# Stores of the experts' results issued from GpSimd instead of ScalarE, in a two-layer mixer with a mixture of experts

## The chip, the cores and the metric

The kernel runs on one core of one Trainium2 chip. The metric is the device time of one execution in microseconds (us); of several executions the median is taken.

## What is computed

The reference is a two-layer network over 256 latent and 256 context tokens of width 1024. Each layer has a mixer (convolution, chunked recurrence, linear recurrence) and then a mixture of 16 experts; the change concerns the mixture alone. Each token has two experts, chosen inside one of four groups:

```python
expert_id = g_sel[:, None] * EXPERTS_PER_GROUP + top_i          # 2 of 16 for each token
combine = jnp.sum(jax.nn.one_hot(expert_id, N_EXPERTS) * top_w[..., None], axis=1)
for e in range(N_EXPERTS):
    ye = (jax.nn.silu(hf @ w_gate[e]) * (hf @ w_up[e])) @ w_down[e]
    y = y + combine[:, e:e + 1] * ye
```

All is float32. One expert has three weight matrices of 2 MB each. Layer 0 sends 512 tokens through the mixture (64 an expert on average), layer 1 only the 256 latent ones (32 an expert).

## The kernel before

**Work of one expert.** `moe(l, hs, fill)` (line 1086) sorts the tokens and then runs a loop over 16 experts (line 1584) in a fixed order. For an expert the kernel multiplies the gathered tokens with the gate and up matrices (`gu`, matmul at line 1356), copies the PSUM result to `gs` (`evac`, line 1373 on ScalarE), transposes and activates it (`act`, lines 1379, 1382, 1391), and multiplies with the down matrix (`down`, line 1404). Each expert has room for 128 tokens in two halves: half 0 holds tokens 0 to 63, half 1 tokens 64 to 127, and work that no token needs is skipped on TensorE by a branch.

**Stores.** For 15 of the 16 experts `store(x, b, ps, n_s)` (line 1466) follows each half of `down`: ScalarE (half 0) or VectorE (half 1) copies PSUM into a tile `Y` (line 1468; three buffers in all), and one or two DMAs write `Y` to the tensor `Yd` in memory (line 1472). That makes three DMAs an expert and 90 over both layers. The first of an expert is always done; the other two carry the condition that the expert has more than `s0` tokens. The number `n_s` is loaded into a register of the issuing engine (line 1597). The DMAs are issued by ScalarE, in its instruction order. The sixteenth expert is kept out of `Yd`.

**Loads.** SyncE (SP) issues all weight loads, in a fixed order (`ahead`, `ewt`, lines 1114 to 1140: a tile of 1 MB at line 1128, two of 512 KB at line 1122), up to 12 tiles ahead in layer 0 and 15 in layer 1. A load waits until TensorE has finished with the tile whose place it takes. It neither reads nor writes `Y` or `Yd`.

**Fetch.** In the last expert's turn `fetch` (line 1543) lets GpSimd issue indirect DMAs that read each token's two rows back from `Yd` (8 in layer 0, 4 in layer 1, line 1554). They need all stores of the layer landed. `take` (line 1566) then weighs and adds the rows (ScalarE line 1570, VectorE lines 1573 and 1575, GpSimd line 1576); `spread_y` (line 1448) and a matmul (lines 1462, 1709) add the sixteenth expert. In layer 1 GpSimd also loads `fin` (line 1589).

**Order.** TensorE's order is the program's own. The order on the other engines is set by a scheduler in the framework, which also places all semaphore waits and hands each DMA the semaphore that tells of its landing.

Of the kernel before, what the change touches and what calls it, by code (L numbers as in the profile page):

```python
# [39 lines left out]
def hybrid_kernel(ctx, tc, x, c, cx, c_ctx, w_mod, b_mod, norm1_g, norm2_g, w_in, conv_w, conv_b, conv_ln_g,  # L40
# [3 lines left out]
    nc = tc.nc  # L44
# [11 lines left out]
    Yd = dram.tile([NE - NPE, P, D], F32, name="Yd", tag="Yd")  # L56
    cnt = [0]

    def bank(shape=(P, 512)):
        cnt[0] += 1  # L60
        return box["ps"].tile(list(shape), F32, tag="ps", name=f"ps{cnt[0]}", bufs=box["nps"])
# [141 lines left out]
    def wsplit(w, a):  # L203
        r = wpair(w, a)
        for hf in range(2):
            whalf(*r, hf)
        return r[1:]
# [878 lines left out]
    def moe(l, hs, fill):  # L1086
# [4 lines left out]
        with tc.tile_pool(name=f"mo{l}", bufs=1, reuse_waits="tile") as mo, \  # L1091
# [7 lines left out]
            def mt(name, shape, dt=F32, tag=None, bufs=1):  # L1099
                return mo.tile(list(shape), dt, name=f"{name}{l}", tag=tag or name, bufs=bufs)  # L1100
# [121 lines left out]
            def onehot(pr):  # L1222
                P2 = tmp.tile([P, NT, 256], F32R, "t4" if last else "q4", f"P2_{l}_{pr}")
                for j in range(2):
                    e = ORDER[2 * pr + j]
                    for i in range(NT):
                        V.tensor_scalar(P2[:, i, j * P:j * P + P], iota1, pm1[:, i, e:e + 1], None, op0=OP.is_equal)
                if last or pr % 2 == 0:
                    XT = tmp.tile([P, KC, 256], F32, "t8", f"XT{l}_{pr}")
                else:  # L1230
                    XT = kt([P, KC, 256], name=f"XT{l}_{pr}", tag="B")
                st[pr] = XT, P2
# [57 lines left out]
            cnti = mt("cnti", [P, NE + 1], I32)  # L1290
# [52 lines left out]
            def load_w(x):  # L1343
                g0, u0, g1, u1, d0, d1 = wt[6 * x:6 * x + 6]
                return [g0, g1, u0, u1, d0, d1]


            def gu(x, b, ps, ws, c=0):
                XT = st[x // 2][0]
                w, q = (64, 512) if b is None else (32, 256)  # L1350
                c0 = (x % 2) * P + (c if b is None else 32 * b)
                o0 = 256 * ((b or 0) % 2)
                for k in range(KC):
                    for t in range(P // w):
                        g, f0 = (t, 0) if b is None else (t // 2, 256 * (t % 2))
                        T.matmul(ps[w * t:w * t + w, o0:o0 + q], XT[:, k, c0:c0 + w],  # L1356
                                 ws[2 * g + k // 4][k % 4][:, f0:f0 + q], start=(k == 0), stop=(k == KC - 1))


            def by32(x, b):  # L1360
                return last and b == 0 if last or x in pec else b == 1

            def evac(x, b, ps):

                gs = tmp.tile([P, 512], F32, "t2", f"gs{l}_{x}_{b}")
                o, src = gs.rearrange("t (h k p) -> t h k p", h=2, k=2), ps.rearrange("t (h p k) -> t h k p", h=2, k=2)
                if x in pec and not by32(x, b):
                    V.tensor_scalar(o, src, Wc[:, x, 2 * b:2 * b + 1], None, op0=OP.mult)  # L1368
                elif x in pec:
                    V.tensor_tensor(o, src, Wc[:, x, 2 * b:2 * b + 2].unsqueeze(2).unsqueeze(3)  # L1370
                                    .to_broadcast([P, 2, 2, P]), op=OP.mult)
                else:
                    S.copy(o, src)  # L1373
                return gs
# [91 lines left out]
            def store(x, b, ps, n_s):  # L1466
                Y = tmp.tile([P, 512], F32, "Y", f"Y{l}_{x}_{b}")
                (V.tensor_copy if b else S.copy)(Y, ps)  # L1468
                w, q = (32, 256) if by32(x, b) else (64, 512)
                for c in range(64 // w):  # L1470
                    s0 = 64 * b + w * c
                    nc.scalar.dma_start(Yd[x, s0:s0 + w, :].rearrange("s (h f) -> h s f", f=q), Y[:, q * c:q * c + q],
                                        **({"cond": n_s > s0} if s0 else {}))

            def overflow():
# [67 lines left out]
            def fetch():  # L1543

                Yf = Yd.rearrange("e s d -> (e s) d")
                for i in range(NT):
                    if last:
                        yas.append(mt(f"ya{i}", [P, 2, D], tag=("vh", "vl")[i]))
                    else:
                        if i % 2 == 0:  # L1550
                            ya = mt(f"ya{i}", [P, 2, 2, D], tag=("vh", "vl")[i // 2])
                        yas.append(ya[:, i % 2])
                    for cc in range(2):
                        G.indirect_dma_start(out=yas[i][:, cc, :], out_offset=None, in_=Yf,  # L1554
                                             in_offset=bass.IndirectOffsetOnAxis(ap=rowi[:, cc, i:i + 1], axis=0),
                                             bounds_check=(NE - NPE) * P - 1, oob_is_err=False)
# [27 lines left out]
            for x in range(NE):  # L1584
                e = ORDER[x]
                ws = load_w(x)
                if last and x == NE - 2:
                    fin = tmp.tile([P, 2, D], F32, "t8", "fin")
                    nc.gpsimd.dma_start(fin[:, 0], final_g.partition_broadcast(P))  # L1589
                pr = x // 2 + 1  # L1590
                more = pr < NE // 2
                if more and x % 2 == 0:
                    onehot(pr)
                n_e = n_next
                wide = x in pec
                if not wide:
                    n_s = nc.values_load(cnti[0:1, e:e + 1], engines=(mybir.EngineType.Activation,), min_val=0,
                                         max_val=NTOK)
                else:
                    fetch()  # L1600
                    if not last:
                        box["w0"] = [wsplit(w_in[1], a) for a in (0, 256)]
                        Z[1:] = [bank()]
                        V.memset(Z[1], 0.0)
                pa = X1 or bank()

                if last:
                    gu(x, 0, pa, ws)
                    if wide:
                        prep(x)  # L1610
                    with tc.If(n_e > 32):  # L1611
                        gu(x, 1, pa, ws)
                else:
                    gu(x, None, pa, ws)
                    if wide:
                        prep(x)
                    else:
                        with tc.If(n_e > 64):
                            gu(x, 2, X2, ws)
                ga = evac(x, 0, pa)  # L1620
                if more:
                    gather(pr, 2 * (x % 2))
                if last or wide:
                    with tc.If(n_e > 64):
                        gu(x, None, X2, ws, 64)
                else:
                    with tc.If(n_e > 96):
                        gu(x, 3, X2, ws)
                gb = evac(x, 1, X2)
                hA = act(x, 0, ga)  # L1630
                hB = act(x, 1, gb)
                if yas:
                    take(*gate((0, 1)))
                if more:
                    gather(pr, 2 * (x % 2) + 1)
                if x + 1 < NE:
                    n_next = count(x + 1)
                if wide:
                    down_w(0, hA, ws)
                    with tc.If(n_e > 64):  # L1640
                        down_w(1, hB, ws)
                elif last:
                    down(0, hA, Y1, ws)
                    with tc.If(n_e > 32):
                        down(1, hA, Y1, ws)
                    store(x, 0, Y1, n_s)
                    with tc.If(n_e > 64):
                        down(None, hB, Y2, ws)
                    store(x, 1, Y2, n_s)
                else:  # L1650
                    py = bank()
                    down(None, hA, py, ws)
                    store(x, 0, py, n_s)
                    with tc.If(n_e > 64):
                        down(0, hB, Y2, ws)
                        with tc.If(n_e > 96):
                            down(1, hB, Y2, ws)
                    store(x, 1, Y2, n_s)
                ahead(x + 1)
                if x == OVER:  # L1660
                    gr = gate_rows(l, 5, mo, "gr", range(NT // 2), NT // 2)
                    overflow()
# [127 lines left out]
```

## Time and profile before

| | |
|---|---|
| median of 3 runs | 1248.26 us (1246.55 to 1252.63) |
| profiled execution | 1250.44 us |
| its span in the trace | 1248.7 us |
| TensorE busy | 1068.6 us, 86% of the span |
| VectorE, ScalarE, GpSimd busy | 541.1, 362.9, 192.9 us |
| expert loop of layer 0, some | 340 to 690 us |
| expert loop of layer 1, some | 957 to 1210 us |

The span is the time from the first to the last instruction of the profiled execution; its own time has 1.7 us more around it. PE is TensorE's matmul, PEld its weight load, DVE is VectorE, ACT ScalarE, POOL GpSimd, SP SyncE; a q behind the name means the engine's sequencer, which issues DMAs and waits without counting as busy. L1472 is line 1472. A tile's buffer number is left out: `w` stands for every weight tile.

### The profile page before, as it was taken

What the parts mean: (1) busy time and instruction counts of PE and PEld (TensorE: products, weight loads), DVE (VectorE), ACT (ScalarE), POOL (GpSimd) and SP (SyncE); (2) the same over time, 40 slices, a digit from 0 to 9 for tenths busy, and PEclk for the clock granted to TensorE, in tenths of its full rate; (3) what the DMA queues carried; (4) which work ended last, traced back from release to release, by engine and by line L of the source; (5) the groups of instructions that cost most, each with busy time, mean ns of one, the idle gap of its engine ahead of it and who ended that gap; (6) DMA issues with size and microseconds to landing.
All of it is one profiled execution on the core that took longest, in us unless ns stands there. A gap on an engine that the chain in (4) does not pass through costs nothing. (4 is left out here: it accounts for less than half of the span.)

```text
span 1248.7 us, 21479 instructions
## 1 busy us (share of the span) xinstructions
PE 1068.6 (86%) x8655; PEld 726.6 (58%) x8655; DVE 541.1 (43%) x1239; ACT 362.9 (29%) x713; POOL 192.9 (15%) x151
## 2 busy tenths in 40 slices
PE   6899798999899899999897498989888968868676
PEld 4577697899654454555343167788776644434332
DVE  3779958832811111111012999937844110111005
ACT  3554255442321111111010354545433221111102
POOL 3411214332000000000002541113420000000012
PEclk9999999999999899999999698989999989988868
DMA  9636642675978787866886452346697989878981
GB/s 317 199 102 201 229 135 69 197 264 194 361 280 318 283 308 281 336 253 251 335 321 244 162 154 68 119 152 210 230 371 279 389 328 400 345 279 333 360 300 72
DMA packets 137304, 313.08 MB, mean 251 GB/s; under 512 B 15700, under 2 KB 101504, under 8 KB 117328
## 3 DMA queue, kind: packets, MB, share of 16 engines
q1 hardware_dynamic: 128896, 295.74, 64.2%
q10 hardware_dynamic: 6048, 8.43, 1.8%
q0 software_dynamic: 2224, 6.95, 1.5%
q8 instruction: 102, 1.67, 0.5%
q14 instruction: 34, 0.28, 0.1%
HBM read 298.25 MB, written 20.71 MB: 255 GB/s over the span
## 5 line engine op out<-in xcount | busy, mean ns | idle before, releaser
L1356 PE MATMUL X<-w,XT 128*32 128x256 f32 (+1 forms) x2016 | 158.1, 432 | 47.4 <-DMA w<-in_w_up_dram 29.0
L1391 DVE TENSOR_TENSOR hT<-sg,ps 128x256 f32<-128x256 f32 x63 | 24.7, 421 | 342.5 <-ACT sg L1382 342.2
L1356 PEld LDWEIGHTS X<-w,XT 128*32 128x32 f32 (+1 forms) x2016 | 78.4, 120 | 124.3 <-issue 45.3
L1356 PE MATMUL ps<-w,XT 128*64 128x512 f32 x512 | 122.7, 619 | 16.4 <-PEq L1478 5.2
L1356 PEld LDWEIGHTS ps<-w,XT 128*64 128x64 f32 x512 | 44.0, 142 | 91.1 <-issue 63.7
L1242 PE MATMUL ps<-P,vh 128*128 128x256 f32 x336 | 88.8, 300 | 4.8 <-PEq L1611 3.5
L1242 PE MATMUL ps<-P,vl 128*128 128x256 f32 x336 | 83.7, 285 | 0.0
L1373 ACT COPY gs<-X 128x512 f32<-128x512 f32 x45 | 26.0, 587 | 192.7 <-PE X L1356 75.8
L756 DVE SCALAR_TENSOR_TENSOR acc<-cb,cwh,acc 128x512 f32<-128x512 f32 (+1 forms) x120 | 81.3, 715 | 1.0
L1242 PEld LDWEIGHTS ps<-P,vh 128*128 128x128 f32 x336 | 65.2, 194 | 21.0 <-issue 10.9
L1468 DVE COPY Y<-Y 128x512 f32<-128x512 f32 x30 | 20.7, 692 | 129.2 <-DMA Yd<-Y 47.5
L1554 POOL DMA_INDIRECT ya<-Yd,rowi x12 | 12.6, 1049 | 388.5 <-issue 357.5
L1242 PEld LDWEIGHTS ps<-P,vl 128*128 128x128 f32 x336 | 65.2, 194 | 0.0
L1404 PE MATMUL Y<-w,hT 128*32 128x256 f32 (+1 forms) x912 | 58.5, 392 | 2.6 <-DMA w<-in_w_down_dram 1.3
L225 PE MATMUL ps<-w,cS 128*32 128x256 f32 x768 | 49.5, 397 | 9.8 <-DMA w<-in_w_mod_dram 9.5
L1404 PE MATMUL ps<-w,hT 128*64 128x512 f32 x240 | 54.8, 598 | 0.4 <-DVE hT L1391 0.3
L1379 PE MATMUL ps<-blob,gs 128*128 128x128 f32 x256 | 41.7, 292 | 12.7 <-ACT gs L1373 7.7
L1373 ACT COPY gs<-ps 128x512 f32<-128x512 f32 x15 | 8.8, 587 | 143.4 <-PE ps L1356 106.8
L1404 PEld LDWEIGHTS Y<-w,hT 128*32 128x32 f32 (+1 forms) x912 | 29.7, 112 | 28.7 <-issue 8.7
L1379 PEld LDWEIGHTS ps<-blob,gs 128*128 128x128 f32 x256 | 28.1, 145 | 28.3 <-ACT gs L1373 17.3
L225 PEld LDWEIGHTS ps<-w,cS 128*32 128x32 f32 x768 | 22.8, 113 | 30.5 <-DMA w<-in_w_mod_dram 10.2
L1589 POOL DMA_DIRECT2D fin<-in_final_g_dram x1 | 0.6, 647 | 250.6 <-ACT gs L1373 250.6
(892 smaller groups left out, 2095.9 us busy)
## 6 DMA issues: line engine op xcount, KB each, us to landing
w<-in_w_down_dram SPq DMA_DIRECT2D x58, 1024.0 KB
w<-in_w_gate_dram SPq DMA_DIRECT2D x49, 1024.0 KB
w<-in_w_mod_dram SPq DMA_DIRECT2D x48, 1024.0 KB
w<-in_w_up_dram SPq DMA_DIRECT2D x48, 1024.0 KB
w<-in_w_in_dram SPq DMA_DIRECT2D x23, 1024.0 KB
w<-in_w_up_dram SPq DMA_DIRECT2D x32, 512.0 KB
w<-in_w_gate_dram SPq DMA_DIRECT2D x30, 512.0 KB
w<-in_w_out_dram SPq DMA_DIRECT2D x8, 1024.0 KB
```

What stands on the lines that cost most here:

```text
L225: T.matmul(ps[32 * j:32 * j + 32, hf * 256:hf * 256 + 256], cS[:, k, :], w[:, k, :], start=(k < 4), stop=(k >= 4))
L756: V.scalar_tensor_tensor(acc[:, ch], src, wcol, acc[:, ch], op0=OP.mult, op1=OP.add)
L1242: T.matmul(ps[:, cc, :], v[:, i, k * P:k * P + P], P2[:, i, :], start=(n == 0), stop=(n == 2 * NT - 1))
L1356: T.matmul(ps[w * t:w * t + w, o0:o0 + q], XT[:, k, c0:c0 + w], ws[2 * g + k // 4][k % 4][:, f0:f0 + q], start=(k == 0), stop=(k == KC - 1))
L1373: S.copy(o, src)
L1379: T.transpose(pt[:, f, :], gs[:, f * P:f * P + P], ident)
L1391: V.tensor_tensor(hT, sg, pt[:, :, 64:128], op=OP.mult)
L1404: T.matmul(ps[w * t:w * t + w, o0:o0 + q], hk, ws[4 + k // 2][k % 2][:, q * t:q * t + q], start=(k == 0), stop=(k == 3))
L1468: (V.tensor_copy if b else S.copy)(Y, ps)
L1554: G.indirect_dma_start(out=yas[i][:, cc, :], out_offset=None, in_=Yf, in_offset=bass.IndirectOffsetOnAxis(ap=rowi[:, cc, i:i + 1], axis=0) ...
L1589: nc.gpsimd.dma_start(fin[:, 0], final_g.partition_broadcast(P))
```

## The change

The 90 stores are issued by GpSimd, and the register with the token count is loaded on GpSimd. Copies, conditions, sizes and addresses stay.

```diff
@@ -1469,7 +1469,7 @@
                 for c in range(64 // w):
                     s0 = 64 * b + w * c
-                    nc.scalar.dma_start(Yd[x, s0:s0 + w, :].rearrange("s (h f) -> h s f", f=q), Y[:, q * c:q * c + q],
+                    nc.gpsimd.dma_start(Yd[x, s0:s0 + w, :].rearrange("s (h f) -> h s f", f=q), Y[:, q * c:q * c + q],
                                         **({"cond": n_s > s0} if s0 else {}))
@@ -1594,7 +1594,7 @@
                 if not wide:
-                    n_s = nc.values_load(cnti[0:1, e:e + 1], engines=(mybir.EngineType.Activation,), min_val=0,
+                    n_s = nc.values_load(cnti[0:1, e:e + 1], engines=(mybir.EngineType.Pool,), min_val=0,
                                          max_val=NTOK)
```

## Rows read from the trace of the kernel before

**Rows 1.** Busy time by stage: start:end, length, busy time (x instructions), granted clock, DMA share, GB/s.
```profile
340.00:690.00 350.00, 318.36 (x2230) 164.95 (x2228) 53.61 (x138) 52.47 (x102) 10.70 (x10) 0.97 0.75 294
...
957.00:1210.00 253.00, 194.30 (x2264) 113.92 (x2264) 34.34 (x76) 41.70 (x86) 1.78 (x3) 0.89 0.86 338
```
**Rows 2.** Waits of PE, 957 to 1210: total us, times, longest us.
```profile
PE X L1356 <- DMA w<-in_w_up_dram: 29.0, 15, 3.6
...
PE ps L1379 <- ACT gs L1373: 4.7, 3, 3.4
...
PE Y L1404 <- DMA w<-in_w_down_dram: 1.3, 1, 1.3
```
**Rows 3.** Waits of PE, 340 to 690.
```profile
PE ps L1356 <- DMA w<-in_w_up_dram: 3.8, 3, 2.1
...
PE ps L1379 <- ACT gs L1373: 2.1, 1, 2.1
...
PE ps L1356 <- DMA w<-in_w_down_dram: 0.3, 1, 0.3
```
**Rows 4.** Waits of SP's queue, 957 to 1210.
```profile
SPq L1128 <- DMA Yd<-Y: 68.8, 7, 13.4
SPq L1122 <- DMA Yd<-Y: 66.1, 7, 16.4
...
SPq L1128 <- DMA w<-in_w_gate_dram: 24.7, 10, 9.2
...
SPq L1122 <- DMA w<-in_w_up_dram: 6.6, 4, 2.3
```
**Rows 5.** Waits of SP's queue, 340 to 690.
```profile
SPq L1128 <- DMA Yd<-Y: 79.9, 5, 17.8
SPq L1122 <- DMA Yd<-Y: 61.6, 5, 18.1
SPq L187 <- DMA Yd<-Y: 21.1, 1, 21.1
```
**Rows 6.** Timeline of SP near the end of layer 1: start, length, instruction.
```profile
1179.39 0.33 SPq L1128 DMA_DIRECT2D w<-in_w_gate_dram  x1
1194.97 1.14 SPq L1122 DMA_DIRECT2D w<-in_w_up_dram  x2
```
**Rows 7.** DMA in 957 to 1210: rate in 40 equal slices; ScalarE's queue.
```profile
GB/s 339 246 420 421 260 424 378 131 311 410 417 420 417 417 402 350 417 400 141 415 421 156 201 318 233 427 417 416 239 394 248 296 424 330 316 395 424 236 286 196
...
q10 hardware_dynamic: 2770, 2.88, 3.3%
```
**Rows 8.** The stores' line: duration ns min/median/max on the issuing queue.
```profile
L1472 ACTq DMA_DIRECT2D Yd<-Y x90: 138/181/6956, 360.3 to 1197.7; - x90
```
**Rows 9.** Timeline of ACT at the end of layer 0's experts.
```profile
653.90 0.59 ACT L1468 COPY Y<-ps 128x512 f32<-128x512 f32 x1 [3.56 <-PE ps L1404]
666.09 4.14 ACTq L1472 DMA_DIRECT2D Yd<-Y  x3
...
682.91 1.15 ACT L1570 ACTIVATE ya<-ya,ws 128x1024 f32<-128x1024 f32 x1 [7.80 <-DMA ya<-Yd,rowi]
```
**Rows 10.** Timeline of POOL, 600 to 700, first and last fetch of layer 0.
```profile
677.14 1.16 POOL L1554 DMA_INDIRECT ya<-Yd,rowi  x1 [354.45 <-issue]
...
686.80 0.99 POOL L1554 DMA_INDIRECT ya<-Yd,rowi  x1 [0.30 <-issue]
```
**Rows 11.** Timeline of PE behind the last expert of layer 0.
```profile
696.95 5.21 PE L1462 MATMUL ps<-yt,PT 128*128 128x512 f32 x8 [14.80 <-DVE yt L1448]
```
**Rows 12.** The fetch's line: duration ns, and time from issue to landing.
```profile
L1554 POOL DMA_INDIRECT ya<-Yd,rowi x12: 987/993/1376, 677.1 to 1212.5; - x12
...
DMA to landing us min/median/max: 5.5/8.8/9.7
```
**Rows 13.** Timeline of POOL in layer 1: a direct DMA issued there.
```profile
1176.89 0.65 POOL L1589 DMA_DIRECT2D fin<-in_final_g_dram  x1 [250.64 <-ACT gs L1373]
```
**Rows 14.** Timeline of ACT at the end of layer 1's experts.
```profile
1226.21 2.19 ACT L1570 ACTIVATE ya<-ya,ws 128x1024 f32<-128x1024 f32 x2
```

## The prediction

> **What bounds the kernel now.** I read the busy time by stage first. In layer 0's expert loop TensorE is busy for 318 of 350 us at a granted clock of 0.97; in layer 1's for only 194 of 253 us at 0.89 [rows 1]. So layer 0 is held by TensorE, and layer 1 by something else. The waits of TensorE name it: in layer 1 three rows of weight loads, 29.0 the largest and 1.3 the smallest, make 38.6 us together, and the copy `gs` on ScalarE 4.7 us [rows 2]. In layer 0 the three load rows make only 6.0 us and `gs` 2.1 [rows 3].
>
> Is the memory path full, then? Its rate in layer 1 is 338 GB/s on average [rows 1], but slice by slice it jumps between some 420 and 131 [rows 7]. A full path would be flat, so the loads are begun too late. The waits of SP's queue tell why. In layer 1, 134.9 us of SP's time end with the landing of a store, `DMA Yd<-Y` (68.8 and 66.1), and six rows that end with an earlier load, 24.7 the first and 6.6 the last, make 72.4 [rows 4]. In layer 0, 162.6 us end with a store [rows 5]. A load touches neither `Y` nor `Yd`. The one tie I see is the framework's landing semaphores: loads of SP and stores of ScalarE seem to get theirs from one set, in turn, and who reuses one waits for its last DMA. One place shows the price: SP issues a load at 1179.39 and the next only at 1194.97 [rows 6].
>
> ScalarE pays too. The last store of layer 0 has its copy done at 654.5 and is issued at 666.09 [rows 9]. The fetch, which needs it landed, starts at 677.14 [rows 10], `take` waits 7.8 us for it [rows 9], and TensorE stands idle for 14.8 us behind the last expert [rows 11].
>
> **The change, part by part.**
>
> 1. *ScalarE loses 90 issues.* The median is 0.18 us, the longest 6.96 [rows 8]. All the path sees of this is `gs` late for TensorE: 4.7 us in layer 1, 2.1 in layer 0 [rows 2, 3]. I take **-6** of 6.8. The cover of the rest is ScalarE's idle time (41.7 us busy of 253 [rows 1]).
>
> 2. *GpSimd gains 90 issues and 30 register loads.* The trace has no store and no conditional DMA there. From below, ScalarE's 0.18 us an issue [rows 8]; from above, 0.65 for a direct load [rows 13] or 1.0 for an indirect one [rows 12]. I take 0.65, the nearest in kind: 2 us an expert, against intervals of some 17 us (253 us for about 15). GpSimd is idle for 354 us before layer 0's fetch [rows 10] and works 1.8 of 253 us in layer 1 [rows 1], so this costs nothing. Without that cover it would be 90 x 0.65 = 58 us. Queued behind a store that waits for its copy are only the next store, `fin` and the fetch; `fin` is not needed before the end.
>
> 3. *SP no longer waits for stores,* if GpSimd's DMAs have semaphores of their own. What is late next is a tile's place, still in TensorE's use, or an earlier load. Stores are 134.9 of SP's 207 us of DMA waits in layer 1, 65% [rows 4]. So up to 25 of the 38.6 us would go; I take half, 19, since a wait that goes often uncovers another. Bounds: nothing, and all 38.6 [rows 2]. As a check, the stage's bytes (253 us at 338 GB/s) at the plateau of 417 GB/s [rows 7] need 205 us, and the stage without load and `gs` waits lasts 253 - 43 = 210; two limits so close never mesh fully, and 253 - 19 - 4 = 230 leaves 20 us for that. In layer 0, half of 6.0: 3. Together **-22**. The lower clock of layer 1 may come back in part (0.89 against 0.97 [rows 1]); I count nothing for it.
>
> 4. *The moved bytes.* They stay; only their queue changes. ScalarE's queue takes 3.3% of 16 DMA engines' time in layer 1 [rows 7]. That is 8.3 of the stage's 253 us, and it is paid before and after: zero. The Trainium skill's page "DMA: Bandwidth & Descriptors" (Why a DMA increments its semaphore by 16 and not by 1) says that a hardware-issued DMA runs on as many engines as its slowest dimensions allow, the lowest-numbered ones, and a GpSimd one on all or on a rotating set. By it these stores, whose outermost dimension is 2 or 4 blocks, now load the same two or four engines each time: 3.3% of sixteen is 13% of four, so moving them could by itself give up to 10% of layer 1's stage, an estimate of 25 us, about what step 3 gives by the waits. No row here shows single engines; the sum is without it.
>
> 5. *The end of layer 0.* Issued when its copy is done (654.5), the last store lands between 5.5 and 11 us later: the first is the fastest GpSimd DMA [rows 12], the second what the old one took until the fetch began (666.09 to 677.14 [rows 9, 10]). I take 9, near the median of 8.8. The fetch then starts at about 664, not 677. Its eight issues take 10.7 us [rows 10], and the last lands 8.8 later, at about 683 instead of 696. TensorE ended its own work 14.8 us before 696.95, at 682 [rows 11]. So that idle time falls to 2 to 4 us: **-11**, with bounds of 0 and 14.8.
>
> 6. *The end of layer 1.* `take` starts at 1226.2 [rows 14]; TensorE arrived there late because of weights. When these come sooner, the fetch may be next: stores issued until about 1198, landed at 1207, four fetches to 1212, landed at 1221. That is 5 us of room, which step 3 may use up: **+1**, bounds 0 and 5.
>
> Sum: -6 - 22 - 11 + 1 = **-38 us** on the profiled execution's 1250.4, so 1212; that execution lies 2.2 us above the median, so on the median it is **1210**.
>
> **Rivals.**
>
> *A. SP trades one wait for another.* A wait for several things is put down to the last; if the tile's place comes free within a microsecond of the store, nothing is won there. For it: in layer 0 the path loses only 6.0 us in spite of 162.6 us of such waits [rows 3, 5]. Against: the gap in [rows 6], and a rate that falls to 131 GB/s. Then steps 1 and 5 alone remain, -17: **1231**.
>
> *B. Only issue time is saved.* If stores on GpSimd share the semaphores with the loads, steps 3 and 5 go, and step 1's 6.8 us is the most: **1242 to 1248**, in other words that the change does not do what it says. The Trainium skill's page "DMA: Bandwidth & Descriptors" (Issuing engines are not separate DMA queues) says just this: DMAs of all issuing engines run on the same 16 engines, and issuing from several saves only the sequencer's time, usually little. [Rows 4] speak against it, since there the cost of sharing is a wait and not bandwidth.
>
> *C. Slower: the three `Y` buffers.* Half 1 of an expert is copied into the buffer that the previous expert's half 0 had, so a store has to land within about one interval, 17 us. Software-made stores in the full stream could take longer; SP's longest wait for a ScalarE store was already 18.1 us [rows 5]. From 17 us on, each microsecond more is paid in each of some 14 intervals of layer 1. At 20 us that is +42, and with steps 1 and 5 gone some **1285**. Against it: GpSimd's DMAs land in at most 9.7 us [rows 12].
>
> **How the numbers follow.** Forecast 0.62, from 1190 to 1225; a still larger gain 0.04; A 0.19; B 0.08; C 0.07. The low end, 1190, takes all 25 us of step 3, 6 in layer 0, 6.8, 14.8 and 5 for the clock, 58 in all. The high end is A with its step 5 down to half, 1237. Left out are C, B and the largest gains, 0.2. What a measurement can tell here from no change is 0.5%, 6.2 us. Faster than 1242 are the forecast, the larger gain, A and a little of B: 0.87. Within 6.2 us is the rest of B: 0.07. Slower is C, a little less: 0.06.
>
> **What would show it.** SP's rows must have no `DMA Yd<-Y` in either layer, and layer 1's rate must be flatter and its stage shorter than 240 us; load waits of TensorE fall to about 20 us there (step 3). No `gs` wait of over 1 us on TensorE (step 1). The first fetch of layer 0 starts within 12 us of the last copy into `Y`, and the 14.8 us of idle time fall under 5 (step 5). Store issues on GpSimd of 0.5 to 1 us (step 2). Wrong would be: SP's waits move to tiles' places one for one (A), stay with `Yd<-Y` (B), or the copies into `Y` wait for stores by 40 us and more in layer 1 (C).

## The result, and the profile after

The changed kernel takes **1192.01 us** (median of 4 runs, 1189.1 to 1192.86) against 1247.4 of the kernel before (1245.75 to 1252.63), measured on the same chip: a ratio of 0.9545, 95% interval [0.9512, 0.9578]. The forecast was 1210, its range 1190 to 1237: the sign is right and the time lies 2 us inside the range's low end, but the gain is 55 us where 38 were forecast. The profiled execution is 1189.1 us with a span of 1187.5, 61.2 less than before. That is 6 us more than the medians differ by: before's profiled execution lay 3 us above its median, and this one 3 us below.

Where did the 61 go? I cut both traces at TensorE's own work, so that each stretch holds the same instructions: from the first gate and up matmul of a layer to the end of the last expert's down matmuls in layer 0, and to their start in layer 1. First the kernel before, layer 0 and layer 1 (columns as in [rows 1]):

```profile
343.00:681.00 338.00, 314.21 (x2199) 161.65 (x2199) 46.19 (x120) 47.70 (x97) 3.18 (x3) 0.97 0.74 291
946.00:1226.00 280.00, 218.67 (x2514) 126.72 (x2510) 40.07 (x96) 46.25 (x95) 4.71 (x5) 0.89 0.84 328
```

The same two stretches of the kernel after:

```profile
343.00:667.00 324.00, 306.58 (x2200) 159.28 (x2200) 50.98 (x125) 51.85 (x101) 28.15 (x55) 0.99 0.83 312
923.00:1166.00 243.00, 199.27 (x2514) 122.28 (x2510) 40.14 (x96) 46.48 (x95) 19.97 (x50) 0.96 0.95 378
```

Layer 1 lost 37 us. TensorE's idle time in it fell from 61.3 to 43.7 (length less PE's busy time), which is 17.6. The other 19.4 are *busy* time: 2,514 matmuls both times, at a mean granted clock (the share of full speed that TensorE was given) of 0.89 before and 0.96 after. Layer 0 lost 14: 6.4 idle and 7.6 busy. By part, in us of the profiled pair:

| part | forecast | measured |
|---|---|---|
| layer 0's experts | -5 | -14 (idle -6.4, busy -7.6) |
| idle time behind layer 0's experts | -11 | -8.0 |
| layer 1's experts | -23 | -37 (idle -17.6, busy -19.4) |
| end of layer 1 | +1 | -1 |
| mixers and start | 0 | -1 |

The waits of TensorE in layer 1 after the change (923 to 1166; total us, times, longest), against [rows 2]:

```profile
PE ps L1242 <- PEq L1611: 8.1, 9, 2.1
...
PE X L1356 <- DMA w<-in_w_up_dram: 6.3, 5, 2.4
...
PE Y L1404 <- issue: 4.0, 4, 1.3
PE ps L1379 <- PEq L1624: 3.4, 2, 1.9
...
PE X L1356 <- DMA w<-in_w_gate_dram: 2.1, 3, 1.3
...
PE ps L1379 <- ACT gs L1373: 1.0, 2, 0.8
```

The load waits fell from 38.6 to 8.4, further than the forecast's 20. The idle time fell by less than they did, since other rows grew: TensorE now meets its own sequencer at the branches that skip work (L1611 had 3.5, L1624 nothing). In layer 0 no load row is left.

SP's waits, longest rows in layer 0 (340 to 668):

```profile
SPq L1128 <- PEq L1627: 72.6, 6, 12.2
SPq L1122 <- PEq L1627: 58.1, 7, 9.0
SPq L1128 <- PEq L1656: 39.4, 6, 6.8
```

and in layer 1 (915 to 1149):

```profile
SPq L1128 <- PEq L1624: 47.9, 8, 10.8
...
SPq L1128 <- DMA w<-in_w_gate_dram: 17.8, 12, 2.6
SPq L1128 <- DMA w<-in_w_up_dram: 17.6, 10, 3.2
SPq L1128 <- DMA w<-in_w_down_dram: 15.3, 13, 3.2
```

No row with a store is left, where [rows 4] had 134.9 us and [rows 5] 162.6. In layer 0 waits for the place of a tile took over: rows that end with PE or PEq, TensorE done with what the place held before. The rate of layer 1 after (923 to 1166, 40 slices):

```profile
GB/s 127 327 373 422 410 415 419 405 403 408 410 413 408 417 408 409 417 410 422 417 414 384 408 406 422 406 419 406 409 415 405 410 420 413 405 392 306 150 283 0
```

Compare [rows 7]: the dips to 131 and 141 are gone until the last loads. Layer 1's loads now run at the plateau that the slices of before only touched, some 410 GB/s. Its bytes (243 us at 378 GB/s) need 224 us at that rate, an estimate, and TensorE is busy for 199: the two limits lie close together, and no run separates them.

The rows for the moved work, on GpSimd's line and in its timeline at the end of layer 0, and TensorE behind the last expert:

```profile
L1472 POOL DMA_DIRECT2D Yd<-Y x90: 44/52/913, 360.7 to 1141.3; - x90
```
```profile
643.99 0.80 POOL L1472 DMA_DIRECT2D Yd<-Y  x2 [12.83 <-ACT Y L1468]
645.05 0.04 POOL L1472 DMA_DIRECT2D Yd<-Y  x1 [0.26 <-DMA Yd<-Y]
654.85 1.12 POOL L1554 DMA_INDIRECT ya<-Yd,rowi  x1 [9.76 <-issue]
...
664.09 1.50 POOL L1554 DMA_INDIRECT ya<-Yd,rowi  x1 [0.30 <-issue]
```
```profile
674.76 6.08 PE L1462 MATMUL ps<-yt,PT 128*128 128x512 f32 x8 [6.75 <-DVE yt L1448]
```

An issue on GpSimd is 0.04 us when its condition says no, 0.7 to 0.9 when it is done. The fetch of layer 0 starts 22 us earlier than in [rows 10]; TensorE waits 6.75 us behind its last expert instead of 14.80 [rows 11].

### The profile page after: what moved, and what is told of

Read it like the earlier page. It is cut to its first block, busy times and chain, and to the rows that moved or that the text cites. A ratio compares the mean times of both kernels' runs of the same rounds, so it can differ in the third digit from the quotient of the medians.

```text
span 1187.5 us, 21557 instructions
## 1 busy us (share of the span) xinstructions
PE 1040.2 (88%) x8655; PEld 718.5 (61%) x8655; DVE 541.1 (46%) x1239; ACT 363.4 (31%) x713; POOL 227.7 (19%) x241
## 5 line engine op out<-in xcount | busy, mean ns | idle before, releaser
L1356 PE MATMUL X<-w,XT 128*32 128x256 f32 (+1 forms) x2016 | 138.1, 398 | 22.9 <-PEq L1647 6.4
L1472 POOL DMA_DIRECT2D Yd<-Y x90 | 33.4, 386 | 518.9 <-ACT Y L1468 462.8
L1356 PEld LDWEIGHTS X<-w,XT 128*32 128x32 f32 (+1 forms) x2016 | 75.7, 113 | 84.1 <-issue 38.4
L1356 PE MATMUL ps<-w,XT 128*64 128x512 f32 x512 | 115.9, 605 | 11.3 <-PEq L1478 5.9
L1379 PE MATMUL ps<-blob,gs 128*128 128x128 f32 x256 | 42.0, 290 | 10.8 <-PEq L1624 3.4
L1379 PEld LDWEIGHTS ps<-blob,gs 128*128 128x128 f32 x256 | 27.7, 144 | 26.7 <-issue 15.5
L1382 ACT ACTIVATE sg<-ps 128x256 f32<-128x256 f32 x64 | 24.2, 391 | 43.4 <-PE ps L1379 26.8
```

Of the source, the lines that this page charges most:

```text
L1379: T.transpose(pt[:, f, :], gs[:, f * P:f * P + P], ident)
L1382: S.activation(sg, pt[:, :, 0:64], AF.Silu)
L1472: nc.gpsimd.dma_start(Yd[x, s0:s0 + w, :].rearrange("s (h f) -> h s f", f=q), Y[:, q * c:q * c + q], **({"cond": n_s > s0} if s0 else {}))
```

## The experiments

Two theories stood against each other for the 37 and 14 us. **S**: loads and ScalarE's stores share landing semaphores, and SP waits for a store where it reuses one. **E**: a store whose outermost dimension has 2 or 4 blocks runs on few of the 16 DMA engines, so it lands late and delays the loads there. The runs that add a DMA write it to a scratch tensor, `Sd`; no kernel leaves work out. The diffs show the lines that matter; the scratch tensor's declaration, continuation lines that only move, and the engine of the register load are left out. Each ratio is to the kernel before, measured on the same chip.

**1. Landing semaphores alone: `gp_tiny_sc`.** After, with three 1 KB DMAs an expert added on ScalarE, to a scratch tensor.

```diff
                     nc.gpsimd.dma_start(Yd[x, s0:s0 + w, :].rearrange("s (h f) -> h s f", f=q), Y[:, q * c:q * c + q],
                                         **({"cond": n_s > s0} if s0 else {}))
+                    nc.scalar.dma_start(Sd[l, x, (s0 - 32 * (not last and s0 > 0)) // 32], Y[0:16, 0:16])
```

> The stores stay on GpSimd as in the change; ScalarE issues three further DMAs an expert behind the same copies, 1 KB each, to a tensor that nobody reads. They bring no load worth naming, but take landing semaphores of the loads' set at the places where the stores had them. Theory S (loads wait on semaphores shared with stores): SP's rows with a DMA of Y come back, over 60 us in layer 1, and 15 to 40 of the 55 us won are lost, 1207 to 1232 us. Theory E (a store issued by ScalarE runs on two or four DMA engines only, so it lands late and makes the loads on these engines late): under 5 us lost, 1190 to 1197.

Measured: 1209.4 us (1208.06 to 1210.58), ratio to before 0.9676 [0.9638, 0.9714]. SP waits for the tiny DMAs as it did for the stores (its queue in layer 1, 922 to 1185; the line numbers are higher by the lines added):

```profile
SPq L1129 <- DMA Sd<-Y: 51.9, 10, 12.8
SPq L1123 <- DMA Sd<-Y: 48.7, 8, 13.3
```

A load touches neither `Y` nor `Sd`, and 1 KB is no traffic: 45 of them are 45 KB in a stage of 263 us. So the tie is the semaphores. The traces, which number each DMA's landing semaphore, show it too: before, SP's loads and ScalarE's 90 stores use the same eight; after, GpSimd's DMAs use eight others. And a wait for a semaphore is not only a wait for a transfer: of SP's 100.6 us here, 43 passed before the tiny DMA had even been issued, because ScalarE was not yet at it. Layer 1 went from 243 to 263 us (12 of it idle, 8 busy; TensorE's waits for `gs` on ScalarE are only 1.9 of the 12). Layer 0 stayed at 324, although SP waited 78 us there for the tiny DMAs too. So sharing with DMAs that land soon (in 1.4 to 7.4 us) costs some 20 us in layer 1 and nothing in layer 0.

**2. The conditional stores alone on ScalarE: `cond_sc`.** Before, with the unconditional store on GpSimd.

```diff
+                    eng = nc.scalar if s0 else nc.gpsimd
-                    nc.scalar.dma_start(Yd[x, ...
+                    eng.dma_start(Yd[x, ...
```

> Of the three stores of an expert the first, which is always done, is issued by GpSimd, the two conditional ones by ScalarE as before; the skipped ones among them move nothing. Theory S: two thirds of the shared semaphores are back, so SP waits for stores again and the time is 1205 to 1235. Theory E: only the executed conditional stores are back on few engines, a third to a half of the bytes in layer 1 and a fifth in layer 0: 1195 to 1210.

Measured: 1218.9 us (1214.82 to 1220.67), 0.9741 [0.9699, 0.9784]. All of the loss is in layer 1 (270 us); layer 0's experts stay at 324. Two of three stores, often skipped, cost as much there as three tiny DMAs and 7 us more. The trace shows that a skipped DMA still takes its turn at a semaphore: SP's longest wait for a store, 20.0 us, ended 0.1 us after a store that took 0.147 us, as the skipped ones do (the done ones take 0.55 or more). It also shows that ScalarE pays: TensorE's waits for `gs` are 11.4 us in layer 1, 1.0 in after, and the longest, 9.7, comes where ScalarE itself stood 13 us in front of a store, until an earlier one on that store's semaphore had landed.

**3. Each layer alone: `gp_l1_only` and `gp_l0_only`.** The stores are on GpSimd in one layer, on ScalarE in the other.

```diff
+                    eng = nc.gpsimd if last else nc.scalar        # gp_l1_only
+                    eng = nc.gpsimd if not last else nc.scalar    # gp_l0_only
```

> Layer 0's stores stay on ScalarE, layer 1's go to GpSimd. If the two stages are independent: layer 1's 37 us of the trace are won and layer 0's 22 are not, 1209 to 1217.

> Layer 0's stores go to GpSimd, layer 1's stay on ScalarE. If the two stages are independent: some 22 us are won, 1225 to 1232.

Measured: 1214.16 us, 0.9684 [0.9664, 0.9704], and 1227.36 us, 0.9804 [0.9782, 0.9825]. The gains, 3.2% and 2.0%, together are 5.1% where the whole change has 4.6% (4.2 to 4.9): each layer's gain stands by itself, and neither needs the other.

**4. Another shape on either engine: `sc_split` and `gp_split`.** Each store is cut by its column blocks into 2 or 4 DMAs, whose outermost dimension is then 64 or 32 rows; 10 DMAs an expert instead of 3.

```diff
+                    for h in range(D // q):
+                        nc.scalar.dma_start(Yd[x, s0:s0 + w, q * h:q * h + q], Y[w * h:w * h + w, q * c:q * c + q],
+                                            **({"cond": n_s > s0} if s0 else {}))
```

> All stores on ScalarE as before the change, but each is cut along the column blocks into two or four DMAs of 64 or 32 rows, so that none has an outermost dimension of 2 or 4; the data are the same, the DMAs 10 instead of 3 an expert. Theory E: stores land in some 5 us and no engine carries more than another, so most of the gain comes without GpSimd: 1195 to 1215. Theory S: over three times as many stores on the shared semaphores, 1240 to 1290.

> The change, with each store cut in the same way into two or four DMAs. Theory E, if GpSimd's stores too still run on few engines: they land sooner (14 to 18 us now in layer 0), layer 0's end wins 2 to 6 us, 1184 to 1191. Theory S: nothing left to win, 1190 to 1196. If ten issues an expert are dear for GpSimd: up to 1200.

Measured: `sc_split` 1257.0 us, 1.0063 [1.0034, 1.0092]; `gp_split` 1185.87 us (1183.41 to 1190.72), 0.9501 [0.9459, 0.9543]. On ScalarE the two layers went opposite ways: layer 0's experts 331 us instead of 338 and the idle time behind them 5.4 instead of 14.8, layer 1 300 instead of 280. The shape helped layer 0 on ScalarE itself, without GpSimd; in layer 1 the many DMAs went through the shared semaphores. On GpSimd, layer 1 took 238 us instead of 243. The intervals of `gp_split` and the change overlap, but four traces with GpSimd's whole stores in layer 1 and none of ScalarE's (after, `gp_l1_only`, `sp_few`, `sp_spread`) have 243 us there, and the two with cut ones (`gp_split`, `mix`) 238.

**5. The shape by itself: `sp_few` and `sp_spread`.** After, with one more store an expert, of constants to a scratch tensor, issued by SP. The same bytes in both; the written pattern is 2 (or 4) blocks in the one, 128 rows in the other.

```diff
+                            nc.sync.dma_start(Sd[l, x, 0:r, :].rearrange("s (h f) -> h s f", f=q), blob[:, 0:q])    # sp_few
+                            nc.sync.dma_start(Sd[l, x, 0:r, :].rearrange("s (h f) -> (s h) f", f=q), blob[:, 0:q])  # sp_spread
```

> The change, and after each expert's last load SP issues one further DMA that nobody waits for: it writes a constant tile to a tensor nobody reads, 256 KB in layer 0 and 128 KB in layer 1, with the stores' shapes, outermost dimension 2 and 4. It is issued in the loads' own order and tied to no result. Theory E (stores of that shape issued in hardware use two or four DMA engines and make every load wait for these): layer 0's experts take 6 to 14 us longer, layer 1's 10 to 25, 1205 to 1230 us in all. Theory S alone (only semaphores count): the bytes spread over all engines cost some 0.5 us an expert in layer 1, which uses 99% of the engines now, 1195 to 1203.

> As sp_few, with the same bytes written to 128 rows in a row, so that the outermost dimension is 128. Both theories: 1195 to 1205. The difference of sp_few and sp_spread is what the shape costs: theory E 10 to 30 us, theory S under 3.

Measured: `sp_few` 1242.69 us, 0.9924 [0.9906, 0.9941]; `sp_spread` 1189.19 us, 0.9492 [0.9477, 0.9508]. As a test of the experts this failed: nothing tied these stores to an expert, and the scheduler put all 32 into layer 0's mixer (first issue at 55 us, last at 204), where the 52 us were lost; the expert loops are as in after. But there the shape stands alone in the trace. DMA of `sp_few` from 106 to 147 us:

```profile
DMA  1111111111111111111111111111111111121111
GB/s 52 48 52 52 52 50 50 52 52 52 50 50 52 52 52 50 50 52 52 52 48 52 52 52 52 48 52 52 52 52 48 52 52 52 60 90 66 52 52 61
...
q1 hardware_dynamic: 1115, 2.17, 13.8%
...
Sd<-blob SPq DMA_DIRECT2D x7, 256.0 KB
Sd<-blob SPq DMA_DIRECT2D x3, 128.0 KB
```

And from 202 to 206 us, where only stores of 4 blocks (128 KB) are under way:

```profile
DMA packets 384, 0.38 MB, mean 96 GB/s; under 512 B 9, under 2 KB 384, under 8 KB 384
...
q1 hardware_dynamic: 384, 0.38, 27.2%
```

For the first 34 of these 41 us stores of 2 blocks are nearly all that moves: some 52 GB/s. The whole stretch, with a few of 4 blocks at its end, keeps 13.8% of sixteen engines at work, which is 2.2 engines. With 4 blocks the rate is 96 GB/s and the share 27.2%, 4.4 engines. So the rate follows the number of blocks. The plateau of after is some 410 GB/s, eight times that of 2 blocks, at which a store of 256 KB takes 5 us alone. The same stores as 128 rows, in `sp_spread`, cost no time that can be told from none.

**6. The shape inside the expert loops: `gp_tw_few` and `gp_tw_spread`.** After, with the unconditional store written a second time by ScalarE to a scratch tensor. It reads `Y`, which holds it in its place. One more landing an expert in both; only the written pattern differs.

```diff
+                    if s0 == 0:
+                        nc.scalar.dma_start(Sd[l, x, 0:w, :].rearrange("s (h f) -> h s f", f=q), Y[:, 0:q])    # gp_tw_few
+                        nc.scalar.dma_start(Sd[l, x, 0:w, :].rearrange("s (h f) -> (s h) f", f=q), Y[:, 0:q])  # gp_tw_spread
```

> After, and for each expert one more DMA, issued by ScalarE: the unconditional store is written a second time, to a scratch tensor that nobody reads, in the old shape (outermost dimension 2 blocks of 64 rows in layer 0, 4 blocks of 32 rows in layer 1). Result as before. It adds 2 MB a layer, some 5 us of layer 1 at 400 GB/s, and one shared landing semaphore an expert instead of three. Theory E (a few-block shape loads few DMA engines and lands late): clearly slower than the twin with the spread shape, by 8 us or more, part of it in layer 0, whose experts come back from 324 towards 338 us. Theory S (only the shared semaphores cost): within 3 us of the spread twin, some 1202 to 1210, all in layer 1.

> The same second store, of the same bytes from the same tile, on ScalarE, but written to the scratch tensor row after row (outermost dimension 128 rows). Theory E: near after, 1195 to 1205, with layer 0's experts at 324 us; what is left is the bytes and the shared semaphore. Theory S: like the other twin, 1202 to 1210.

Measured: 1241.84 us, 0.9939 [0.9918, 0.9960], against 1212.83 us, 0.9714 [0.9679, 0.9748]. The shape alone is 29 us. The stages of `gp_tw_few`:

```profile
343.00:677.00 334.00, 311.07 (x2196) 160.61 (x2196) 46.12 (x118) 48.82 (x98) 23.73 (x51) 0.98 0.81 310
940.00:1217.00 277.00, 212.75 (x2514) 123.56 (x2508) 39.94 (x96) 46.45 (x95) 19.98 (x50) 0.90 0.87 338
```

and of `gp_tw_spread`:

```profile
344.00:667.00 323.00, 306.40 (x2198) 159.61 (x2196) 48.48 (x121) 50.14 (x100) 25.68 (x53) 0.99 0.86 322
926.00:1187.00 261.00, 208.86 (x2512) 120.83 (x2504) 39.79 (x96) 46.01 (x94) 19.93 (x50) 0.94 0.92 359
```

Layer 0's experts: 334 and 323 us, where before has 338 and after 324. So the shape alone brings back 11 of the 14 us that the change won there. In layer 1 the few-block twin has 16 us more than the spread one, and the spread one 18 more than after, for its bytes (2 MB, 5 us at 400 GB/s) and the shared landings. With the 20 us of `gp_tiny_sc` for landings alone, the 16 make 36 of the 37 us that the change won in layer 1: S and E have about half each. How the late landing acts in layer 0 shows in the waits, from 340 to 684; SP's queue in `gp_tw_few`:

```profile
SPq L1129 <- DMA Sd<-Y: 130.2, 9, 24.1
SPq L1123 <- DMA Sd<-Y: 42.1, 3, 20.4
```

and, in `gp_tw_spread`, the row of the same line and the time from a twin's issue to its landing in layer 0 (343 to 677):

```profile
SPq L1129 <- DMA Sd<-Y: 79.9, 7, 14.3
```
```profile
DMA to landing us min/median/max: 3.8/8.3/10.6
```

The twins of `gp_tw_few` that something waited for landed 14 to 29 us after their issue, as did before's stores (9 to 30), and of SP's waits for them all but 6 us lie behind the issue. VectorE, too, waited 61.8 us in `gp_tw_few` for a `Y` whose twin had not landed.

The late landing does not cost by itself, though. GpSimd's whole stores in after keep the shape: eight of layer 0's that something waited for landed 10 to 18 us after their issue (six of `gp_split`: 5 to 6), and layer 0 has 324 us all the same. So layer 0 seems to need both for its loss, a late landing and a load or ScalarE's work that has to wait for it; either cure ends it. Whether the few busy DMA engines also slow the loads' own transfers was not separated.

**7. The shape on ScalarE with fewer DMAs: `sc_split0`.** Before, with the unconditional store alone cut: 4 DMAs an expert in layer 0, 6 in layer 1.

```diff
-                    nc.scalar.dma_start(Yd[x, s0:s0 + w, :].rearrange("s (h f) -> h s f", f=q), Y[:, q * c:q * c + q],
+                    for h in range(1 if s0 else D // q):
+                        o, u = (slice(0, P), D // q) if s0 else (slice(w * h, w * h + w), 1)
+                        nc.scalar.dma_start(Yd[x, s0:s0 + w, q * h:q * h + q * u].rearrange("s (h f) -> h s f", f=q),
+                                            Y[o, q * c:q * c + q], **({"cond": n_s > s0} if s0 else {}))
```

> Before (all stores on ScalarE), with the unconditional store alone cut by its column blocks: 2 DMAs in layer 0, 4 in layer 1, each of 64 or 32 rows; the two conditional stores stay whole. 4 and 6 DMAs an expert instead of 3. Theory E: layer 0 gains (its experts from 338 to some 328 us, the idle time behind them under 10), layer 1 is between a small gain and a small loss, since three more DMAs an expert go through the shared semaphores: 1230 to 1245. Theory S: layer 0 unchanged, layer 1 slower: 1250 to 1265.

Measured: 1243.35 us, 0.9933 [0.9901, 0.9965]. Layer 0's experts take 320 us and leave 5.6 idle: all that the change won in layer 0, and 4 us more, with every store still on ScalarE and on the shared semaphores. Layer 1 takes 296 us, 16 more than before, with twice the landings in the shared set.

**8. Each layer with its own cure: `mix`.** Layer 0 as in `sc_split0`, layer 1 as in `gp_split`.

> Layer 0 on ScalarE with only the unconditional store cut by its column blocks (as in sc_split0), layer 1 on GpSimd with every store cut (as in gp_split). Theory: layer 0's loss came from the few-block shape alone and layer 1's mostly from the shared landing semaphores, so each layer needs only its own cure. Layer 0: experts 320 us and 6.5 idle; layer 1: 238 to 243 us; 1181 to 1190 in all, like the two-layer GpSimd version or a little below. If layer 0 needed GpSimd's own semaphores too, its experts would be above 330 us and the whole above 1195.

Measured: 1186.39 us (1183.45 to 1188.61), 0.9488 [0.9471, 0.9505]. Layer 0 has 320 us and 6.7 idle, layer 1 238. It and `gp_split` (0.9501) can't be told apart. Its interval lies below the change's own [0.9512, 0.9578], by under 1%; so does that of `sp_spread` [0.9477, 0.9508], which only adds stores to the change, so this doesn't show that `mix` is faster. Its trace has 4 us less than the change's in layer 0's experts and 5 in layer 1's, and 4 more at the end of layer 1.

## Why the prediction was right, and where it was wrong

The time fell within the range, but by luck in part: its low end held 5 us for the clock, which gave 27, and all that step 3 could win. The mechanism of step 3 was right; two terms were put at nothing.

**Step 1, the issues taken from ScalarE: right.** The `gs` waits were 6.8 us; 1.2 are left (1.0 and 0.2), against a forecast of -6. No single one is over 0.8.

**Step 2, the issues on GpSimd: right.** 0.7 to 0.9 us for one that is done, a little above the 0.65 assumed, and 0.04 for one that is skipped; GpSimd was busy for 20 of layer 1's 243 us, and nothing waits for these issues but the fetch. The 0.18 us taken as a lower bound were those of a skipped store: on ScalarE's queue 46 of the 90 took 0.14 to 0.19 us and the 44 others 0.55 or more.

**Step 3, SP no longer waits for stores: the mechanism right, the sizes not.** `gp_tiny_sc` shows the shared semaphores, and what they cost in layer 1, 20 us, is near what I put there (19), but by chance: 8 of the 20 are busy time, which the step did not count. The idle time of both layers' experts fell by 24.0 us; steps 1 and 3 had 28. But they were to be the whole, and two terms were missing.

**The first is in step 3's last sentence: "I count nothing for" the clock.** It gave back 27 us (19.4 in layer 1, 7.6 in layer 0) of busy time for the same work. One shape of matmul shows it, in layer 1 of before and, below it, in layer 1 of after:

```profile
L1356 PE MATMUL X<-w,XT 128*32 128x256 f32 x1408 | 107.5, 440 | 47.4 <-DMA w<-in_w_up_dram 29.0 <-DMA w<-in_w_gate_dram 8.3 <-PEq L1647 5.7
```
```profile
L1356 PE MATMUL X<-w,XT 128*32 128x256 f32 x1408 | 87.4, 391 | 22.9 <-PEq L1647 6.4 <-DMA w<-in_w_up_dram 6.3 <-PEq L1478 5.7
```

This form alone has 20.1 us less, 49 ns on each of 1,408. The clock has two levels, 2.4 GHz (1.00) and 1.2 GHz (0.50). Sorted by the level that was granted while they ran, 1,052 of these matmuls took 381 ns at 1.00 before and 316 took 632 ns at 0.50 (the rest ran across a change); after, it is 1,348 at 380 and 51 at 634. So the busy time came back through the clock. Short stretches of before show the order of things:

```profile
1180.00:1183.00 3.00, 2.82 (x56) 1.59 (x52) 0.69 (x1) 0.59 (x1) 0.00 (x0) 1.00 0.95 384
1183.00:1186.00 3.00, 1.63 (x28) 0.84 (x20) 0.00 (x0) 0.00 (x0) 0.00 (x0) 1.00 0.97 395
1186.00:1189.00 3.00, 2.08 (x28) 0.98 (x28) 0.00 (x0) 0.00 (x0) 0.00 (x0) 0.86 1.01 425
1189.00:1192.00 3.00, 2.23 (x10) 1.57 (x8) 0.26 (x1) 1.46 (x3) 0.00 (x0) 0.50 1.02 420
```

TensorE was busy for 1.63 and then 2.08 of 3 us, with a wait of 2.29 us for weights between, and then the granted clock was at 0.50. So an idle stretch is paid twice: while it lasts, and on the matmuls behind it. [Rows 1] had the figures from which this could be bounded: 194.30 us busy at 0.89 instead of 0.97 in layer 1 are 16 us too many (194.3 x (1 - 0.89/0.97)). No run held the waits and changed the clock alone; that it follows the waits rests on these rows, and on layer 1 of all fourteen kernels: the six with 39 to 44 us idle have a clock of 0.95 to 0.99, the six with 52 to 64 us one of 0.89 to 0.94, and `sc_split0` and `sc_split`, with 74 and 85 us, 0.87 and 0.88. Within a group the clock does not follow the idle time in order.

**The second is step 4, the moved bytes at zero: wrong.** It is why the waits went further than I let them go: TensorE's load waits in layer 1 are 38.6 us before, 27.9 in `gp_tiny_sc` and 8.4 after. `sp_few` shows 2.2 engines at work for 2 blocks and 4.4 for 4. The Trainium skill's page "DMA: Bandwidth & Descriptors" (Why a DMA increments its semaphore by 16 and not by 1) says that a DMA runs on the largest number of engines, up to 16, that divides the sizes of its slowest dimensions. The trace agrees with that for 2 and 4 blocks; which engines these are it doesn't show. By this rule the prediction had named 25 us for layer 1 and left them out of the sum. The twins put it at 16 us in layer 1, and in layer 0 at 11 us and 2 of the idle time behind. In layer 0 step 3 foresaw 3 us from semaphores; sharing them costs nothing there where the stores land soon (`gp_tiny_sc`, `sc_split0`), and 14 us where they land late. The step had the bytes right (3.3% of sixteen engines) and the wrong divisor.

**Step 5, behind layer 0: right in kind, -8.0 instead of -11.** The fetch started 10.3 us after the last copy into `Y` (654.85 against 644.60), the eight issues took 10.7 us as before, but TensorE reached the end of its own work sooner too: 23.4 us after that copy instead of 27.7. The idle time is 6.75, not under 5. And the step did not ask why the old issue came 11.6 us after the copy [rows 9]. The trace shows that ScalarE waited there for the landing semaphore of a store it had issued at 639.01, 27 us earlier; in `sc_split0` the same store is issued at once, on ScalarE, and the idle time is 5.6.

**Step 6: small, as said, but outside its bounds.** The end of layer 1 was forecast at +1, bounds 0 and 5, and is -1.2. The fetch did not come next: the four issues of the fetch were done 10.8 us before `take` began at 1166.22.

**Rivals.** A's sign appeared in layer 0: SP's 162.6 us of store waits became waits for places of tiles. But A's price did not follow: TensorE's 6.0 us of load waits there went with them, and 7.6 us of busy time. B fell: the Trainium skill's page "DMA: Bandwidth & Descriptors" (Issuing engines are not separate DMA queues) says that another issuing engine saves only sequencer time; here it saved 55 us, of which `gs` accounts for 6, so the measurement stands against it. C fell: in layer 1 copies into `Y` waited 8.0 us for stores, not 40. (Its time is mis-added: 1248 and 42 are 1290, not 1285. Nothing rests on it.)

## What to carry to other kernels

When a queue of loads waits for the landing of a store that it has nothing to do with, put the stores on an engine whose DMAs have landing semaphores of their own; the price is what the loads lose, not the issue time. Before that, look at the outermost dimension of each store: 2 or 4 blocks there left most DMA engines out (52 and 96 GB/s). Cutting the unconditional store into DMAs of 64 or 32 rows, without moving it, won 18 us in the layer held by TensorE and lost 16 in the layer held by its loads, where the extra landings shared their semaphores. And when waits of TensorE are to go, cost the lower clock with them, from the busy time and the granted clock of that stage.

## What the runs showed of the hardware that had not been expected

A store of 2 blocks on a queue by itself moves some 52 GB/s and one of 4 blocks 96, at 13.8% and 27.2% of the 16 DMA engines. A conditional store that is skipped still holds its turn at a landing semaphore, and a load waited 20.0 us for one. Of DMAs issued by GpSimd a skipped one takes 0.04 us, where the fastest on ScalarE's queue took 0.14 [rows 8]. GpSimd's stores, cut finer, moved layer 1 from 243 to 238 us though no semaphore was shared with the loads any more. They land in 5 to 6 us in layer 0 instead of 10 to 18, so their shape counts for the landing on GpSimd as well; how the 5 us come of it was not tested.
